# The gate's sigmoids and the exponentials' table load issued with the gate's sums, and head 1's transposes one unit later, in a hybrid decoder layer on one core

## The chip, the cores and the metric

The kernel runs on one core of one Trainium2 chip. The metric is device time in microseconds (us), the median of several runs; less is better. Beside the runs stands one profiled execution, from which every row of the trace in this document comes. Engines are called as in the profile: PE (TensorE's matmuls), PEld (its weight loads), DVE (VectorE), ACT (ScalarE), POOL (GpSimd), SP (SyncE, which here only issues DMAs).

## The reference, cut to what matters

One decoder layer on 256 tokens of width 1024, all in float32:

```python
h = rms_norm(x, norm1_g)
q, k, v, u = split(h @ w_in)               # 512 + 512 + 512 + 1024 columns
q, k = rope(rms_norm(q)), rope(rms_norm(k))
attn = softmax(mask(q k^T / 8)) v          # 8 heads of 64, causal
a, g = split(u + glu_b)                    # 512 + 512
c = causal_depthwise_conv(a * sigmoid(g))  # 31 taps, + dw_b
c = silu(layer_norm(c))
x = x + concat(attn, c) @ w_out
h = rms_norm(x, norm2_g)
y = x + (silu(h @ w_gate) * (h @ w_up)) @ w_down   # 2816 wide
```

With 256 tokens there is a single attention block, so the selection of blocks selects nothing.

## The kernel before, in words

Matmuls run in fp32r on split numbers. Each weight piece (128 x 1024, `raw`) is split in two: ACT copies it to `wh` (the high part, L289) and DVE subtracts that from it to get `wl` (the low part, L294). A product is three matmuls, high by high, high by low and low by high. SP loads the `raw` pieces in order, and a load waits for its buffer's release by the `wl` before it.

The first projection, `h @ w_in`, is tiled in 5 chunks of 512 columns (k, q, gate g, conv a, v) by 8 row tiles. One row tile of one chunk is a unit: 6 matmuls of 128 x 512 (L745), two token tiles of three products. So there are 40 units; units 25 to 32 belong to chunk 3 (the conv branch a), and a piece of weights serves two units. Each chunk accumulates in two PSUM banks `p`.

The order of the program is the order in which Python issues it, engine by engine. Everything but the projection's matmuls is written as generators, called tasks. Before each unit, `step()` resumes all tasks that are due, in the order in which they were spawned, and `feed()` issues the next `wh` and `wl`. `yield n` means: go on n units later; `yield 0` goes on in the same call. So these numbers decide what stands ahead of what in each engine's queue. The tasks that matter here:

- `spectra_task` (L444): three small matmuls `pw` on PE, one unit apart, each evicted by ACT to `Ws` (L455).
- `gate_task` (L597), spawned when the gate's chunk is done: DVE makes `ug` from the two banks (L602), then after a `yield` ACT does two sigmoids to `sgt` (L606). The next line (L607) is an exponential of a single column, whose purpose is that the table of the exponentials is loaded there.
- `pairs_task` (L545): the scores S of four heads on PE (L554), their mask and maximum on DVE (L562), and the bias `bi` from that (L566). It runs twice, for heads 0 to 3 and 4 to 7.
- `head_task` (L571), one for each head: two exponentials on ACT with the row sums (L576); for an odd head, one unit later, the reciprocal of the sums of a pair and the scaling of both heads' p on DVE (L583, L587); after another `yield` (L590, which reads `LATE` and `EVEN_T`) three transposes `pT` on PE (L593) and their eviction `pTs` on ACT (L595). The transposes use two PSUM banks in turn.
- `conv_task` (L609): `ua`, the folded sums and their split `hh`, `hl` on DVE and ACT (L615 to L629), and the spectrum `hf` on PE (L641, with the matmuls of `mm3` at L312 to L314).

After the projection follow attention times v (`O`, L764), the inverse transform and layer norm (`ln_task`), the output projection (`po`) and the feed-forward layer, whose matmuls are at L781.

`LATE` and `EVEN_T` are:

```python
EVEN_T = (4, 3, 4, 3)
LATE = (5,)
```

Of the kernel before, what the change touches and what calls it, by code (L numbers as in the profile page):

```python
# [39 lines left out]
HF_WAIT = 3  # L40
LN_WAIT = 2
EVEN_T = (4, 3, 4, 3)
Y_ENG = lambda nc: nc.vector
CV_FIRST = 1
WRAP_WAIT = 1
# [9 lines left out]
QT_WAIT = 2  # L55
KT_WAIT = 3
S_WAIT = 4
LATE = (5,)
SECOND = 3
SCORES = 8  # L60
SCRATCH = 8192
# [145 lines left out]
def _build(nc, tc, t, ctx):  # L207
# [12 lines left out]
    def t_bank(name, tag="t"):  # L220
        return psum.tile([P, 512], F32, name=name, tag=tag, bufs=2)

    def work(name, tag, bufs, shape=(P, W), dt=F32):
        return early.tile(list(shape), dt, name=name, tag=tag, bufs=bufs)
# [346 lines left out]
    def head_task(h):  # L571
# [9 lines left out]
        if h % 2:  # L581
# [7 lines left out]
            p = unscaled[h]  # L589
        yield (3 if h in LATE else 2) if h % 2 else EVEN_T[h // 2]  # L590
        b = t_bank(f"pT{h}")
# [5 lines left out]
    def gate_task(banks):  # L597
        G["sg"] = early.tile([P, NT, W], F32, name="sgt", tag="sg")
        us = []
        for i in range(NT):  # L600
            u = work(f"ug{i}", "tmp", 6)
            nc.vector.scalar_tensor_tensor(u, banks[i], rstd1[:, i:i + 1], G["glub"][:, 1, :], op0=ALU.mult, op1=ALU.add)  # L602
            us.append(u)
        yield 2
        for i in range(NT):
            nc.scalar.activation(G["sg"][:, i, :], us[i], AF.Sigmoid)  # L606
        nc.scalar.activation(table, one, AF.Exp)  # L607

    def conv_task(banks):  # L609
# [36 lines left out]
        for j in range(2):  # L646
            pa, pb = (work(f"y{a}{j}", "tmp", 6) for a in "ab")
            nc.vector.tensor_tensor(pa, hf[0], Ws[:, j, :], op=ALU.mult)
            nc.vector.tensor_tensor(pb, hf[1], Ws[:, 1 - j, :], op=ALU.mult)
            Y_ENG(nc).tensor_tensor(Y[j], pa, pb, op=(ALU.subtract, ALU.add)[j])  # L650

# [77 lines left out]
    spawn(tables_task(), CG_STEP)  # L729
    spawn(spectra_task(), SPECTRA)  # L730
    after = (k_task, q_task, gate_task, conv_task, None)
    unit = 0
    for chunk in range(5):
# [357 lines left out]
```

## Time and profile before

| | us |
|---|---|
| median of 3 runs | 281.49 (281.35 to 281.60) |
| profiled execution | 281.06 |
| its span, first to last instruction | 279.3 |
| PE busy | 273.8 |
| DVE busy | 240.4 |
| ACT busy | 189.5 |

The clock granted to TensorE was 1.000 over the span. A row of the timeline has the start and the duration in us, the engine, the line, the operation, output and inputs, shapes, and the count of instructions that are merged in it (x2); in brackets the idle time of the engine before it and what released it. A row of the waits reads: who waited for whom, us in total, how often, the longest. A row of the windows has the stretch, its length, then the busy time of PE, PEld, DVE, ACT and POOL with counts, the granted clock, the DMA share and GB/s.

### The profile page before, as it was taken

The numbers are of one execution on the slowest core, as the hardware profiler recorded it, in microseconds if no ns is written. First come the engines' busy times: TensorE is split into PE (matmuls) and PEld (weight loads), VectorE is DVE, ScalarE is ACT, GpSimd is POOL, SyncE is SP. The second block draws the span as 40 slices with busy tenths as digits, with TensorE's granted clock in tenths as the row PEclk, the third lists the DMA queues.
The fourth block names the chain that finished last, engine by engine and source line by source line (L and its number), as shares of the span: only waits on it lengthen the run. The fifth ranks groups of instructions, "written<-read, shape, count | busy, mean of one in ns | idle before, by whom it ended". The sixth has DMA issues, their size and how long they took to land.

```text
span 279.3 us, 3699 instructions
## 1 busy us (share of the span) xinstructions
PE 273.8 (98%) x1298; PEld 223.8 (80%) x1298; DVE 240.4 (86%) x346; ACT 189.5 (68%) x280; POOL 31.8 (11%) x59
## 2 busy tenths in 40 slices
PE   8999999899999999999999999999999999999995
PEld 5788877688788888888888888888888888888884
DVE  4999998899889957999998999899998999978412
ACT  4967767999769778655887469766687468954300
POOL 0005465002000000011200112002110022000000
PEclk9999999999999999999999999999999999999999
DMA  7999968565506887439999699997599985910012
GB/s 234 393 420 350 410 226 239 182 217 170 228 0 242 336 323 305 180 134 221 253 301 347 224 223 193 367 425 204 98 199 426 394 159 97 329 50 0 2 50 100
DMA packets 13378, 64.59 MB, mean 231 GB/s; under 512 B 1776, under 2 KB 2768, under 8 KB 7856
## 3 DMA queue, kind: packets, MB, share of 16 engines
q1 hardware_dynamic: 10144, 54.80, 51.5%
q0 software_dynamic: 2928, 9.43, 18.8%
q8 instruction: 10, 0.16, 0.2%
q10 hardware_dynamic: 288, 0.14, 0.2%
q14 instruction: 8, 0.07, 0.1%
HBM read 63.05 MB, written 1.05 MB: 230 GB/s over the span
## 4 chain that ended last, share of the span: by engine, by line
PE 94%; ACT 3%; DMA 1%; DVE 1%; issue 0%
PE pd L781 21%; PE p L745 18%; PE U L781 16%; PE fg L781 12%; PE po L781 8%; PE V L781 8%; PE W L781 4%; PE aT L862 2%; DMA first<-w 1%; PE pT L593 1%; PE O L764 1%; ACT p L576 1%; ACT wh L289 1%; PE x2T L804 1%; PE S L554 1%; ACT L607 0%
## 5 line engine op out<-in xcount | busy, mean ns | idle before, releaser
L289 ACT ACTIVATE wh<-raw 128x1024 fp32r<-128x1024 f32 x114 | 118.0, 1057 | 37.1 <-DVE raw L288 19.9
L294 DVE TENSOR_TENSOR wl<-raw,wh 128x1024 fp32r<-128x1024 f32 x114 | 136.1, 1221 | 6.5 <-ACT wh L289 5.6
L781 PE MATMUL pd<-wh,act 128*128 128x512 f32 (+1 forms) x176 | 57.2, 390 | 0.0
L781 PEld LDWEIGHTS pd<-wh,act 128*128 128x128 f32 x176 | 32.9, 188 | 6.6
L781 PE MATMUL pd<-wl,act 128*128 128x512 f32 (+1 forms) x88 | 33.9, 386 | 0.0
L745 PE MATMUL p<-wh,xh 128*128 128x512 f32 x80 | 32.5, 406 | 0.2 <-ACT wh L375 0.2
L302 POOL DMA_DIRECT2D raw<-w x16 | 14.0, 876 | 155.5 <-PE fg L781 58.5
L745 PE MATMUL p<-wh,xl 128*128 128x512 f32 x80 | 31.4, 393 | 0.0
L781 PE MATMUL fg<-wh,g 128*128 128x512 f32 x96 | 30.4, 391 | 0.0
L745 PE MATMUL p<-wl,xh 128*128 128x512 f32 x80 | 26.2, 390 | 0.0
L781 PE MATMUL U<-wh,g 128*128 128x512 f32 x64 | 21.5, 393 | 0.0
L781 PEld LDWEIGHTS fg<-wh,g 128*128 128x128 f32 x96 | 18.0, 188 | 3.7
L288 DVE TENSOR_TENSOR raw<-raw,raw 128x1024 f32<-128x1024 f32 x16 | 19.5, 1221 | 0.1
L781 PEld LDWEIGHTS pd<-wl,act 128*128 128x128 f32 x88 | 16.6, 188 | 3.2
L781 PE MATMUL fg<-wl,g 128*128 128x512 f32 x48 | 18.7, 390 | 0.0
L745 PEld LDWEIGHTS p<-wh,xh 128*128 128x128 f32 x80 | 15.0, 188 | 4.5 <-ACT wh L375 1.2
L745 PEld LDWEIGHTS p<-wh,xl 128*128 128x128 f32 x80 | 15.0, 188 | 3.3 <-DVE xl L370 0.4
L745 PEld LDWEIGHTS p<-wl,xh 128*128 128x128 f32 x80 | 15.0, 188 | 3.2
L865 ACT ACTIVATE act<-aT 128x512 fp32r<-128x512 f32 (+1 forms) x12 | 6.7, 560 | 12.9 <-PE aT L862 12.9
L781 PEld LDWEIGHTS U<-wh,g 128*128 128x128 f32 x64 | 12.0, 188 | 2.4
L781 PE MATMUL po<-wh,mixh 128*128 128x512 f32 x32 | 12.6, 395 | 0.0
L781 PE MATMUL po<-wh,mixl 128*128 128x512 f32 x32 | 12.5, 390 | 0.0
(202 smaller groups left out, 442.5 us busy)
## 6 DMA issues: line engine op xcount, KB each, us to landing
raw<-w SPq DMA_DIRECT2D x43, 1024.0 KB, 7.1
raw<-w POOLq DMA_DIRECT2D x16, 512.0 KB, 6.9
first<-w SPq DMA_DIRECT2D x8, 384.0 KB, 6.3
raw<-w SPq DMA_DIRECT2D x4, 512.0 KB, 7.0
xtok<-xtok SPq DMA_DIRECT2D x2, 512.0 KB, 8.3
x<-xtok SPq DMA_DIRECT2D x1, 1024.0 KB, 8.4
out<-o SPq DMA_DIRECT2D x3, 256.0 KB, 2.0
c_glub<-glub SPq DMA_DIRECT2D x1, 512.0 KB, 11.6
```

What stands on the lines that cost most here:

```text
L288: nc.vector.tensor_tensor(src, src, blocks[add][:, cut(a)], op=ALU.add)
L289: nc.scalar.activation(dst[0], src, AF.Copy)
L294: nc.vector.tensor_tensor(dst[1], src, dst[0].bitcast(F32), op=ALU.subtract)
L302: nc.gpsimd.dma_start(blocks[to][:, cut(a)], t["w"][HEAD + more - 2][:, cut(a)], accum_op=ALU.add)
L554: nc.tensor.matmul(banks[2 * j + a][:, out], G["qT"][rows, j, q], G["kT"][rows, j, k], start=True, stop=True)
L576: nc.scalar.activation(p[:, spl[i]], sm[:, spl[i]], AF.Exp, bias=bi[:, i:i + 1], scale=scq[:, i, h:h + 1], accum_out=s[:, i:i + 1])
L593: nc.tensor.transpose(b[:, a * P:(a + 1) * P], p[:, a * P:(a + 1) * P], ident)
L745: nc.tensor.matmul(banks[i], (xh, xh, xl)[a][:, kt, sls[i]], w[a % 2], start=kt == 0 and a == 0, stop=kt == KT - 1 and a == 2 - (order[-1] ...
L764: nc.tensor.matmul(o, vs[:, i, h * HD:(h + 1) * HD], G["pT"][h][:, i * T:i * T + T - i * P], start=i == 0, stop=i == 1)
L781: nc.tensor.matmul(bank, l, r, start=start and a == 0, stop=stop and a == 2, skip_group_check=on)
L862: nc.tensor.transpose(b[:, a, :], u[:, a * P:(a + 1) * P], ident)
L865: nc.scalar.activation(hi, b[:, 0:nf, :], AF.Copy)
```

## The change

Two numbers change, one by way of a new name:

```diff
+GLU_Y = 0
...
-LATE = (5,)
+LATE = (1, 5)
...
             us.append(u)
-        yield 2
+        yield GLU_Y
         for i in range(NT):
             nc.scalar.activation(G["sg"][:, i, :], us[i], AF.Sigmoid)
         nc.scalar.activation(table, one, AF.Exp)
```

With `GLU_Y = 0` the gate task doesn't pause between its sums on DVE and its sigmoids on ACT: they are issued in the same unit instead of two units later. With 1 in `LATE`, head 1 pauses 3 units instead of 2 ahead of its transposes (L590). The new name moves every line behind it by one: L606 is L607 in the changed kernel.

On ACT, around the gate task, these rows stood in the queue before (`Ws` are the tap spectra, `wh15` to `wh17` weight pieces, `sgt` the sigmoids, `p0` and `p1` the exponentials of heads 0 and 1):

```order
L455 ACTIVATE Ws_511<-pw0_512 128x512
L455 ACTIVATE Ws_511<-pw1_527 128x512
L289 ACTIVATE wh15_542<-raw7_303 128x1024
L455 ACTIVATE Ws_511<-pw2_552 120x512
L606 ACTIVATE sgt_516<-ug0_517 128x512
L606 ACTIVATE sgt_516<-ug1_519 128x512
L607 ACT_TABLE_LOAD
L607 ACTIVATE table_77<-one_75 128x1
L576 ACTIVATE p0_591,sums_515<-sm0_560,bi0_559,scq_438 128x128
```

On ACT, at the same place, with the change:

```order
L456 ACTIVATE Ws_511<-pw0_512 128x512
L607 ACTIVATE sgt_516<-ug0_517 128x512
L607 ACTIVATE sgt_516<-ug1_519 128x512
L608 ACT_TABLE_LOAD
L608 ACTIVATE table_77<-one_75 128x1
L456 ACTIVATE Ws_511<-pw1_530 128x512
L290 ACTIVATE wh15_545<-raw7_303 128x1024
L456 ACTIVATE Ws_511<-pw2_555 120x512
L577 ACTIVATE p0_591,sums_515<-sm0_560,bi0_559,scq_438 128x128
```

The four instructions of the gate move ahead of the second `Ws`, of `wh15` and of the third `Ws`; what follows them stands as it stood.

On PE, at the last unit of chunk 3 (`p30` and `p31` are its banks; `pT1` and `pT0` the transposes of heads 1 and 0), before:

```order
L745 MATMUL p31_510<-wl15_543,xh_110 128x512
L593 MATMUL pT1_668<-c_ident_168,p1_621 128x128 x3
L745 MATMUL p30_509<-wh15_542,xh_110 128x512
L745 MATMUL p30_509<-wl15_543,xh_110 128x512
L745 MATMUL p30_509<-wh15_542,xl_111 128x512
L745 MATMUL p31_510<-wh15_542,xh_110 128x512
L745 MATMUL p31_510<-wl15_543,xh_110 128x512
L745 MATMUL p31_510<-wh15_542,xl_111 128x512
L593 MATMUL pT0_688<-c_ident_168,p0_591 128x128 x3
```

On PE, at the same place, with the change:

```order
L746 MATMUL p31_510<-wl15_546,xh_110 128x512
L746 MATMUL p30_509<-wh15_545,xh_110 128x512
L746 MATMUL p30_509<-wl15_546,xh_110 128x512
L746 MATMUL p30_509<-wh15_545,xl_111 128x512
L746 MATMUL p31_510<-wh15_545,xh_110 128x512
L746 MATMUL p31_510<-wl15_546,xh_110 128x512
L746 MATMUL p31_510<-wh15_545,xl_111 128x512
L594 MATMUL pT0_682<-c_ident_168,p0_591 128x128 x3
L594 MATMUL pT1_688<-c_ident_168,p1_621 128x128 x3
```

The unit's six matmuls now stand ahead of all six transposes, and head 0 comes before head 1. DVE, POOL and SP have the same rows in the same order.

## The prediction

> **What bounds the kernel now.** I read the page first, then the waits of PE, then the timeline of the three engines around the one long wait. The forecast is 1.2 us less, worked out below.
>
> ```profile
> span 279.3 us, 3699 instructions
> PE 273.8 (98%) x1298; PEld 223.8 (80%) x1298; DVE 240.4 (86%) x346; ACT 189.5 (68%) x280; POOL 31.8 (11%) x59
> PE 94%; ACT 3%; DMA 1%; DVE 1%; issue 0%
> PE warm L359 <- DVE one L341: 1.0, 1, 1.0
> PE pT L593 <- DVE p L587: 0.8, 1, 0.8
> PE p L745 <- ACT wh L375: 0.2, 1, 0.2
> PEld O L764 <- ACT vs L752: 0.4, 1, 0.4
> ```
>
> PE is busy for 98% of the span and the chain that ended last is 94% PE, so time is won only where PE stands still. It waits three times as a matmul engine; two of them are in the start, which the change doesn't touch. The third, 0.83 us, is the wait of the first probability transposes (pT, of head 1) for DVE's scaling of p. The last row is a wait of the weight loads alone, near 71.8 us.
>
> PE around that wait, and two places where transposes follow without one (start, duration, operation):
>
> ```profile
> 53.18 0.61 PE L745 MATMUL p<-wl,xh 128*128 128x512 f32 x2
> 54.63 0.70 PE L593 MATMUL pT<-c_ident,p 128*128 128x128 f32 x3 [0.83 <-DVE p L587]
> 55.40 0.39 PE L745 MATMUL p<-wl,xh 128*128 128x512 f32 x1
> 55.63 0.40 PE L745 MATMUL p<-wh,xl 128*128 128x512 f32 x1
> ...
> 56.32 0.40 PE L745 MATMUL p<-wh,xl 128*128 128x512 f32 x1
> 56.56 0.49 PE L593 MATMUL pT<-c_ident,p 128*128 128x128 f32 x3
> 57.12 0.39 PE L745 MATMUL p<-wl,xh 128*128 128x512 f32 x1
> ...
> 58.05 0.40 PE L745 MATMUL p<-wh,xl 128*128 128x512 f32 x1
> 58.29 0.82 PE L593 MATMUL pT<-c_ident,p 128*128 128x128 f32 x6
> 59.17 0.40 PE L745 MATMUL p<-wl,xh 128*128 128x512 f32 x1
> ```
>
> Why p came late is read from ACT and DVE before it:
>
> ```profile
> 40.30 0.60 ACT L455 ACTIVATE Ws<-pw 128x512 f32<-128x512 f32 x1
> 41.95 0.60 ACT L455 ACTIVATE Ws<-pw 128x512 f32<-128x512 f32 x1 [1.05 <-PE pw L454]
> 42.45 1.05 ACT L289 ACTIVATE wh<-raw 128x1024 fp32r<-128x1024 f32 x1
> 45.28 0.60 ACT L455 ACTIVATE Ws<-pw 120x512 f32<-120x512 f32 x1 [1.78 <-PE pw L454]
> 45.78 1.15 ACT L606 ACTIVATE sgt<-ug 128x512 f32<-128x512 f32 x2
> 46.93 1.28 ACT L607 ACT_TABLE_LOAD   x1
> 48.22 0.20 ACT L607 ACTIVATE table<-one 128x1 f32<-128x1 f32 x1
> 48.33 0.48 ACT L576 ACTIVATE p<-sm,bi,scq 128x128 f32<-128x128 f32 x1
> 49.39 1.05 ACT L289 ACTIVATE wh<-raw 128x1024 fp32r<-128x1024 f32 x1
> 51.40 1.99 ACT L289 ACTIVATE wh<-raw 128x1024 fp32r<-128x1024 f32 x2
> ```
>
> ```profile
> 40.02 1.40 DVE L602 SCALAR_TENSOR_TENSOR ug<-p,c,c_glub 128x512 f32<-128x512 f32 x2
> 45.23 0.17 DVE L566 SCALAR_TENSOR_TENSOR bi<-mx,scq 128x8 f32<-128x8 f32 x1
> 45.31 1.22 DVE L294 TENSOR_TENSOR wl<-raw,wh 128x1024 fp32r<-128x1024 f32 x1
> 47.51 0.29 DVE L562 CUSTOM_DVE_ANT_0 sm<-S,c_mask 128x128 f32<-128x128 f32 x1 [0.98 <-PE S L554]
> 49.85 0.17 DVE L566 SCALAR_TENSOR_TENSOR bi<-mx,scq 128x8 f32<-128x8 f32 x1
> 50.47 1.23 DVE L294 TENSOR_TENSOR wl<-raw,wh 128x1024 fp32r<-128x1024 f32 x1 [0.45 <-ACT wh L289]
> 52.48 1.23 DVE L294 TENSOR_TENSOR wl<-raw,wh 128x1024 fp32r<-128x1024 f32 x1 [0.78 <-ACT wh L289]
> 53.62 0.17 DVE L583 RECIPROCAL rec<-sums 128x4 f32<-128x4 f32 x1
> 53.83 1.01 DVE L587 TENSOR_SCALAR p<-p,rec 128x128 f32<-128x128 f32 x4
> 57.01 0.75 DVE L615 SCALAR_TENSOR_TENSOR ua<-p,c,c_glub 128x512 f32<-128x512 f32 x1
> ```
>
> ACT is idle for 1.05 and 1.78 us between 40.9 and 45.28, waiting for the tap spectra (pw), although the gate's sums (ug) are ready at 41.42. Then it does sigmoids, table load and a dummy exponential, 2.55 us from 45.78 to 48.33, while the scores' bias of the first four heads lies ready since 45.40. The two wh behind the exponentials come late, DVE idles 0.45 and 0.78 us for them, and the reciprocal and the scaling behind those on DVE make PE wait.
>
> **The change part by part: the sigmoids and the table load.** They cost no new instruction: the same four move ahead of the second Ws, piece 15's wh and the third Ws. In the new place the first sigmoid starts at 40.30 + 0.50 (the step from 45.28 to 45.78) = 40.8; the second needs ug at 41.42 and starts near 41.5; at the rows' durations the load runs from 42.1 and the next instruction starts near 43.5. So the second Ws goes from 41.95 to 43.5, wh 15 from 42.45 to 44.0, ending at 45.05. Who waits for these: DVE's wl at 45.31, so 0.26 us is left, and behind that DVE has 0.98 us of idle before the second masks, whose start PE sets. The third Ws stays at 45.28 (PE released it), and the first exponential starts at 45.78, not 48.33: 2.55 us earlier. The second bias, 49.85 + 0.17 = 50.02, is in time for the third head (earlier by 2.55 too, at 50.75). No DMA is issued in the moved code, and SP and POOL keep their order.
>
> DVE then: the wh of pieces 16 and 17, at 49.39 and 51.40, start at 46.84 and 48.85. The wl start at 50.02 and, 1.13 later, 51.15, neither waiting; the reciprocal at 52.28 instead of 53.62, 1.34 us earlier; the scalings at 52.49. Before, the first pT started 0.80 us after the scalings did (53.83 to 54.63), so now one could start at 53.29.
>
> **Its worth on PE.** I measure by starts. The last p matmul before the wait started at 53.18 + 0.22 = 53.40 (two in 0.61, one 0.39), the second one after it at 55.40: 2.00 us. The same stretch with three transposes and no wait is 56.32 to 57.12: 0.80. So the wait costs 1.20 us, not 0.83: the 0.37 more is the emptying and refilling of the array. The Trainium skill (Perfetto Trace Analysis, Tensor Engine Instruction) says that a matmul's end is estimated by the profiler and its start observed. By ends the sum would be 0.83 and the forecast 280.7; by starts it is 1.20, and the trace backs the starts, as the two stretches above differ by 1.20.
>
> **Head 1's transposes a unit later.** Without a wait PE would leave unit 31 at 53.40 + 0.23 = 53.63 (the step is 55.40 to 55.63). Now six matmuls stand first, and pT is reached at 53.63 + 6 x 0.23 = 55.01. With p ready at 53.29, that cover is 1.72 us; without this edit it would be 0.34 us. So I cost the edit at nothing: either part alone removes the wait at this place. Six transposes together instead of twice three: 58.05 to 59.17 is 1.12 us, less two steps of 0.23 is 0.66; singly 0.80 - 0.46 = 0.34, twice 0.68. That is 0.02 saved. ACT must empty both banks before heads 2 and 3, which come at 58.29 - 1.20 = 57.09; the evictions end near 56.3.
>
> **What is late next.** PE comes 1.20 us earlier to everything behind. DVE's next dense stretch must come along:
>
> ```profile
> 56.00:72.00 16.00, 16.00 (x83) 13.03 (x83) 15.65 (x33) 14.75 (x34) 1.99 (x4) 1.00 0.62 220
> 63.38 1.29 DVE L629 TENSOR_TENSOR hl<-uf,hh 128x512 fp32r<-128x512 f32 x2
> 65.33 0.39 PE L313 MATMUL hf<-hl,fwd 128*128 128x512 f32 x1
> ```
>
> DVE is busy 15.65 of 16 us there (third number). It needs PE for ua, at 57.01 before and 55.67 now; chunk 3 ends on PE near 55.2. So it keeps its 1.34 us. The nearest margin is hl: ready at 64.67, used at 65.33, 0.66 us; now 0.66 + 1.34 - 1.20 = 0.80. After 72 us PE shows no wait at all, so the 1.20 us should reach the end.
>
> **The sum.** Profiled execution: 281.06 (span 279.3 and 1.76 around it), less 1.20, is 279.86. It lies 0.43 below the median of the runs, 281.49; from that the forecast is 280.29, so 280.3. The bounds: 0.37 us more if the weight loads' wait at 71.8 goes with ACT's lead (279.9); 0.83 instead of 1.20 if the refill is hidden elsewhere (280.7).
>
> **The rivals.** *DVE stays where it is.* If wh 17 ends after 52.4 as before, the idle 1.23 us survives. Head 1's later place still removes the wait, but hl is then 0.54 us late for PE (0.66 - 1.20), and with 0.37 of refill 0.91 comes back: 281.2. For it: ACT is 14.75 of 16 us busy behind. Against it: it needs wh 17 2.5 us later than worked out.
>
> *Slower: the moved block holds up wh 15.* If wh 15 ended at E, DVE would lose E - 46.29 us (47.51 - 1.22). PE waits for hl when that exceeds 0.80, with 0.37 of refill; the gain of 1.20 is eaten at a loss of 1.63, E = 47.9, against 45.05. At E = 48.8 it is 281.49 - 1.20 + (2.5 - 0.8 + 0.37) = 282.4. The rows speak against it: the table load took 1.28 and the dummy started behind it at once. The Trainium skill (ScalarE: Activation LUTs, What ACT_TABLE_LOAD costs) puts a drain of 1.38 us beside the load; the trace shows none. By that E would be 46.4 and DVE would lose 0.1 us, which the margin of 0.80 covers.
>
> *Half of it:* refill not won or a small wait at heads 2 and 3: 280.7.
>
> **How the numbers follow.** A measurement of this kernel tells 0.2% from no change, 0.56 us. Forecast 280.3: 0.63; half of it: 0.17; DVE stays: 0.13; slower: 0.07. So faster 0.80, same 0.13, slower 0.07. The range runs from the bound 279.9 to the unchanged-DVE case at 281.2 and holds more than 8 in 10.
>
> **What would show it.** Right: the first exponential near 45.8, the DVE reciprocal near 52.3, no idle before pT, six pT in a row near 55.0, and the same steps behind 1.2 us earlier. Wrong: a new PE wait for hl (L313), for pT of heads 2 and 3, or in the FFN; a wl at 45.31 that waits for ACT; or a span shorter by 0.8 or less with no PE idle left.

## The result, and the profile after

| | before | changed |
|---|---|---|
| median, us | 281.45 (7 runs) | 279.97 (7 runs) |
| ratio of the runs | | 0.995 (95% interval 0.9936 to 0.9964) |
| profiled execution | 281.06, span 279.3 | 280.43, span 278.6 |

The change makes the kernel faster by 1.48 us in the medians, 1.0 to 1.8 us by the interval. The forecast was 1.2 us and 280.3. Three executions among the runs of the experiments below (345.8, 396.3 and 463.6 us, at mean granted clocks of 0.76, 0.66 and 0.56) count in the medians, which they move by less than 0.1 us, and not in the ratios.

From the page of the changed kernel, the span, the busy times and the chain that ended last, and from its waits all that PE itself waited for, and the weight loads' wait near 71 us:

```profile
span 278.6 us, 3702 instructions
PE 274.1 (98%) x1298; PEld 224.8 (81%) x1298; DVE 240.2 (86%) x346; ACT 189.4 (68%) x280; POOL 31.7 (11%) x59
PE 96%; DMA 2%; ACT 0%; SPq 0%; DVE 0%; issue 0%; ACTq 0%
```

```profile
PE warm L360 <- DVE one L342: 1.0, 1, 1.0
PEld O L765 <- ACT vs L753: 0.4, 1, 0.4
```

The wait for p is gone and no other has taken its place. (The 0.2 us that PE waited in the start before the change is absent too, but `glu_only` and `late_silu` below have it again.) ACT and DVE have left the chain but for fractions of a per cent.

Rows from the timeline of ACT in the changed kernel, at the moved block (line numbers are one higher than before, and rows in between are left out here and in the next two):

```profile
40.86 0.60 ACT L456 ACTIVATE Ws<-pw 128x512 f32<-128x512 f32 x1
41.35 1.15 ACT L607 ACTIVATE sgt<-ug 128x512 f32<-128x512 f32 x2
42.50 1.28 ACT L608 ACT_TABLE_LOAD   x1
44.38 1.05 ACT L290 ACTIVATE wh<-raw 128x1024 fp32r<-128x1024 f32 x1
45.84 0.60 ACT L456 ACTIVATE Ws<-pw 120x512 f32<-120x512 f32 x1 [0.41 <-PE pw L455]
46.34 0.49 ACT L577 ACTIVATE p<-sm,bi,scq 128x128 f32<-128x128 f32 x1
```

That of DVE:

```profile
45.87 1.22 DVE L295 TENSOR_TENSOR wl<-raw,wh 128x1024 fp32r<-128x1024 f32 x1
50.50 2.36 DVE L295 TENSOR_TENSOR wl<-raw,wh 128x1024 fp32r<-128x1024 f32 x2
52.77 0.17 DVE L584 RECIPROCAL rec<-sums 128x4 f32<-128x4 f32 x1
```

And that of PE:

```profile
53.74 0.62 PE L746 MATMUL p<-wl,xh 128*128 128x512 f32 x2
55.33 0.40 PE L746 MATMUL p<-wh,xl 128*128 128x512 f32 x1
55.56 0.82 PE L594 MATMUL pT<-c_ident,p 128*128 128x128 f32 x6
56.45 0.39 PE L746 MATMUL p<-wl,xh 128*128 128x512 f32 x1
57.61 0.82 PE L594 MATMUL pT<-c_ident,p 128*128 128x128 f32 x6
```

This execution was already 0.56 us later than that of before when it got here (53.74 against 53.18), so steps are compared from there. On the clock of the trace before, the exponentials start at 45.78 (46.34 less 0.56), as forecast, against 48.33; the two wl follow each other without a wait; the reciprocal comes at 52.21 (forecast 52.28); and the second matmul behind head 0's transposes, at 57.12 before, is at 56.45, which is 0.67 earlier on the bare clock and 1.23 earlier from the unit ahead of the wait. The forecast of the step was 1.20 + 0.02. The spans differ by 0.7 us, which with the 0.56 is 1.26: what was won here reached the end.

### The profile page after: what moved, and what is told of

It is laid out like the page before. It is cut to its first block, busy times and chain, and to the rows that moved or that the text cites. A ratio compares the mean times of both kernels' runs of the same rounds, so it can differ in the third digit from the quotient of the medians.

```text
span 278.6 us, 3702 instructions
## 1 busy us (share of the span) xinstructions
PE 274.1 (98%) x1298; PEld 224.8 (81%) x1298; DVE 240.2 (86%) x346; ACT 189.4 (68%) x280; POOL 31.7 (11%) x59
## 3 DMA queue, kind: packets, MB, share of 16 engines
HBM read 63.05 MB, written 1.05 MB: 230 GB/s over the span
## 4 chain that ended last, share of the span: by engine, by line
PE 96%; DMA 2%; ACT 0%; SPq 0%; DVE 0%; issue 0%; ACTq 0%
PE pd L782 21%; PE p L746 19%; PE U L782 16%; PE fg L782 12%; PE po L782 8%; PE V L782 8%; PE W L782 4%; DMA first<-w 2%; PE aT L863 2%; PE S L555 1%; PE O L765 1%; PE pT L594 1%; PE x2T L805 1%; PE cT L722 0%; PE pdlast L782 0%; PE qT L498 0%
```

## The experiments

Each edit is against the changed kernel unless it says otherwise, and each time is against runs of the kernel before on the same chip: with the first four runs a median of 281.51, with the next two 281.25, with the last four 281.27.

**Each part alone.** `glu_only`, the gate's part:

```diff
-LATE = (1, 5)
+LATE = (5,)
```

> Only the gate's part of the change: sigmoids and table load in the same unit, head 1's transposes where they stood. My theory (either part alone removes PE's wait, this one because DVE also gets 1.34 us ahead): the whole gain, 1.2 us less than before, no PE wait at the first pT, a cover of about 0.3 us there. Rival (the later transposes are needed): a wait of some tenths stays at pT and the gain is 0.5 us or less.

Measured: 279.84 us, ratio 0.9944 (0.993 to 0.9958). PE doesn't wait at pT, which starts at 53.78, 1.25 us after DVE began the scalings (52.53). The whole gain is here, and the rival is wrong.

`late_only`, head 1's part:

```diff
-GLU_Y = 0
+GLU_Y = 2
```

> Only head 1's later transposes; the sigmoids two units behind the gate's sums as before. My theory: the wait at pT is gone, but ACT and DVE are not ahead, so hl is ready at 64.67 on the clock of the trace before while PE comes for it at 64.13: a new PE wait of 0.54 us there and 0.37 us of refilling, net gain 0.3 us (0.1 to 0.5). Rival (this part alone does it): 1.2 us less than before and no wait at hf.

Measured: 281.07 us, ratio 0.9993 (0.998 to 1.0005), at most 0.6 us less than before. The size fits my theory, but by luck, since the place does not. The timeline of PE with this part alone, at hf and at the transposes of heads 6 and 7:

```profile
63.68 0.48 PE L313 MATMUL hf<-hh,fwd 128*128 128x512 f32 x1
64.08 0.50 PE L314 MATMUL hf<-hl,fwd 128*128 128x512 f32 x1
64.42 0.40 PE L315 MATMUL hf<-hh,fwd 128*128 128x512 f32 x1
...
67.86 0.39 PE L746 MATMUL p<-wh,xl 128*128 128x512 f32 x1
68.86 0.93 PE L594 MATMUL pT<-c_ident,p 128*128 128x128 f32 x6 [0.61 <-ACT pTs L596]
...
69.86 0.39 PE L746 MATMUL p<-wl,xh 128*128 128x512 f32 x1
```

And that of ACT there:

```profile
65.98 1.28 ACT L580 ACT_TABLE_LOAD   x1
...
67.39 1.04 ACT L290 ACTIVATE wh<-raw 128x1024 fp32r<-128x1024 f32 x1
68.33 0.85 ACT L596 ACTIVATE pTs<-pT 128x384 f32<-128x384 f32 x2
```

At hf the steps are 0.40 and 0.34 us instead of 0.32 and 0.22 as in the trace before: 0.2 us. The larger loss is later. From the last p matmul to the second one behind six transposes is 2.00 us (67.86 to 69.86) against 1.12 without a wait: 0.88. The transposes of heads 6 and 7 need the two banks of heads 4 and 5, and ACT begins to empty those only at 68.33, behind the load of the silu's table and a wh. Together 1.1 of the 1.2 us is lost again.

**Who holds the gain back there?** `late_silu` is `late_only` with the silu's load moved out of that queue:

```diff
 head_task:
-        if h == H - 1:
-            nc.scalar.activation(table, one, AF.Silu)
...
 ln_task:
+        nc.scalar.activation(table, table, AF.Silu)
         yield CV_WAIT
```

> Head 1's later transposes alone, and the load of the silu's table moved from behind the last exponentials (ACT, L579 before) to the layer norm, where ACT idled 2.7 us. In the run with the later transposes alone PE waited at the transposes of heads 6 and 7 for ACT's evictions of heads 4 and 5, 0.8 us by starts, and 0.2 us at hf. Theory (ACT's queue behind the exponentials holds the gain back): the load's 1.4 us leave that queue, the wait at heads 6 and 7 goes, 0.2 us at hf stays, and it is 1.0 us less than before. Rival (DVE's hl holds it, and the wait at heads 6 and 7 only follows from it): still 0.3 us less than before.

Measured: 279.88 us, ratio 0.9953 (0.9938 to 0.9968). ACT's timeline at the same place:

```profile
65.60 1.04 ACT L290 ACTIVATE wh<-raw 128x1024 fp32r<-128x1024 f32 x1
66.55 0.84 ACT L594 ACTIVATE pTs<-pT 128x384 f32<-128x384 f32 x2
68.34 0.87 ACT L594 ACTIVATE pTs<-pT 128x384 f32<-128x384 f32 x2 [0.95 <-PE pT L592]
```

The evictions of heads 4 and 5 now start at 66.55, ACT idles 0.95 us for PE where PE had waited for ACT, and the gain is there with DVE as late as before. So ACT's queue was the holder, and DVE's hl cost only its 0.2 us or a little more.

**One unit instead of none.** `glu_one`:

```diff
-GLU_Y = 0
-LATE = (1, 5)
+GLU_Y = 1
+LATE = (5,)
```

> The gate's sigmoids one unit behind its sums instead of two or none, head 1's transposes where they stood; the block then stands behind the second Ws and ahead of piece 15's wh. My theory: the block fills idle time from about 42.5 to 45.0, wh 15 goes to about 45.0 and ends near 46.1, the exponentials start near 46.6 instead of 48.3, which is early enough: 1.2 us less than before. Rival (only the foremost place is early enough): less than half of it.

Measured: 279.91 us, ratio 0.9952 (0.9934 to 0.9971). The first exponential starts at 46.36 (forecast 46.6). The foremost place is not needed.

**A longer block in the new place.** `sig3`:

```diff
+        for _ in range(3):
+            nc.scalar.activation(G["sg"][:, 1, :], us[1], AF.Sigmoid)
         nc.scalar.activation(table, one, AF.Exp)
```

> The changed kernel with the second sigmoid done three times more, which adds 3 x 0.52 = 1.57 us to ACT's block ahead of the second Ws and piece 15's wh (the result is the same). My theory: wh 15 ends near 46.6 on the clock of the trace before, DVE's wl waits 1.3 us for it, but the 0.98 us of idle ahead of the second masks and the margin of 0.8 us at hl take it: no time lost against the changed kernel, 1.2 us less than before. Rival (every microsecond in front of wh 15 counts): 1.6 us slower than the changed kernel, 0.4 us slower than before.

Measured: 280.36 us, ratio 0.996 (0.9946 to 0.9974). The trace comes from a second set of runs of the same kernel, `sig3_again`:

> The changed kernel with the second sigmoid done three times more, again, for its profile. The repeats take 1.96 us, not 1.57, so wh 15 ends 2.0 us later and DVE's second masks start 0.3 to 0.8 us later. Theory: the margins at the first pT (1.7 us) and at hl (0.8 us) take it, so no wait of over 0.3 us on PE, and 0.9 to 1.2 us less than before. Rival (every microsecond in front of wh 15 counts): 0.8 us slower than before.

Measured: 280.41 us, ratio 0.9966 (0.9952 to 0.998): 0.96 us less than before by the ratio. The three repeats took 1.96 us, 0.65 each, where the two sigmoids ahead of them step at 0.52 (two in 1.14, one 0.62). The repeats all write the same half of `sgt` and those two write different halves; whether that is the reason was not tested. DVE's wl for piece 15 in this run, then PE around the transposes of heads 6 and 7:

```profile
47.55 1.22 DVE L295 TENSOR_TENSOR wl<-raw,wh 128x1024 fp32r<-128x1024 f32 x1 [1.50 <-ACT wh L290]
...
68.39 0.39 PE L748 MATMUL p<-wh,xl 128*128 128x512 f32 x1
68.74 0.92 PE L594 MATMUL pT<-c_ident,p 128*128 128x128 f32 x6
...
69.73 0.40 PE L748 MATMUL p<-wl,xh 128*128 128x512 f32 x1
```

The wl waits 1.50 us for wh 15. On PE, behind the start, only the stretch at heads 6 and 7 is longer, 1.34 us (68.39 to 69.73) instead of 1.12. Two microseconds in front of wh 15 cost these 0.2 us by the trace and some 0.4 by the ratios, whose intervals overlap: the margins take most of it.

`pair`, a further pair of table loads:

```diff
         nc.scalar.activation(table, one, AF.Exp)
+        nc.scalar.activation(table, one, AF.Sigmoid)
+        nc.scalar.activation(table, one, AF.Exp)
```

> The changed kernel with one more pair of table loads behind the gate's (a sigmoid and an exponential of one column, each with its load: 2 x (1.28 + 0.2) = 2.97 us more ahead of the second Ws and piece 15's wh; the result is the same). My theory: DVE loses 1.6 us by then (2.56 us later at wl 15, less the 0.98 us of idle), the transposes of the first heads are just covered, and at hl the margin of 0.8 us is overrun by 0.8 us: with 0.37 us of refilling 1.2 us slower than the changed kernel, about the time of before. Rival 1 (all of it is hidden): the time of the changed kernel. Rival 2 (each switch of tables costs 2.66 us, 1.38 more than its load's row): DVE loses 4.3 us and the kernel is 3 us slower or more than before.

Measured: 281.50 us, ratio 1.0008 (0.9996 to 1.0019), the time of before, which is the number of my theory. ACT's timeline in this run, the three loads up to the second Ws:

```profile
42.94 1.28 ACT L608 ACT_TABLE_LOAD   x1
44.24 0.20 ACT L608 ACTIVATE table<-one 128x1 f32<-128x1 f32 x1
44.46 1.28 ACT L609 ACT_TABLE_LOAD   x1
...
45.98 1.28 ACT L610 ACT_TABLE_LOAD   x1
47.27 0.20 ACT L610 ACTIVATE table<-one 128x1 f32<-128x1 f32 x1
47.38 0.58 ACT L456 ACTIVATE Ws<-pw 128x512 f32<-128x512 f32 x1
```

From load to load is 1.52 us, the load and its dummy, with no drain between. The Trainium skill (ScalarE: Activation LUTs, What ACT_TABLE_LOAD costs) puts 1.38 us of drain beside each; neither this trace nor the time has room for two more of those. PE's loss of 1.2 us is again mostly at the transposes of heads 6 and 7: a wait of 0.64 us for ACT's evictions, 0.9 by starts (69.08 to 71.11 instead of 1.12). At hf and the transposes ahead of it, where I had put all of it, it is 0.3 (64.22 to 65.91 instead of 1.35). That the number came out is luck in part.

**The same block in the old place.** Against the kernel before, the second sigmoid once, twice and three times more (`sig1_old`, `sig2_old`, `sig3_old`):

```diff
+        for _ in range(n):
+            nc.scalar.activation(G["sg"][:, 1, :], us[1], AF.Sigmoid)
         nc.scalar.activation(table, one, AF.Exp)
```

> The kernel before with the second sigmoid done three times more, 1.57 us more ahead of the exponentials (the result is the same). My theory: there the block stands on the path, so PE's wait at the first pT grows from 0.83 to 2.4 us and the kernel is 1.6 us slower than before. Rival (the wait has another cause, a wh or a load): no change, or less than 0.8 us.

> The kernel before with the second sigmoid done once more: 0.65 us more ahead of the exponentials, by the run with three more (which took 1.96 us). Theory (slope of one, and the granted clock falls only after a long wait): PE's wait at the first pT is 1.5 us, the clock stays at 1.0, 0.65 us slower than before. Rival (a wait of more than 0.83 us already costs the clock): 1.5 us slower or more, matmuls behind it at 0.43 us a step.

> The kernel before with the second sigmoid done twice more: 1.3 us more ahead of the exponentials. Theory: PE waits 2.1 us at the first pT. Without a fall of the clock it is 1.3 us slower than before, with one as in the run with three more 2.7 to 3.0 us slower. I expect no fall (1.3), the wait being under 2.5 us.

| added on ACT, us | PE's wait at pT, us | median, us | ratio |
|---|---|---|---|
| 0 | 0.83 | 281.25, 281.27 | 1 |
| about 0.65, once | 1.50 | 282.08 | 1.0023 (1.0011 to 1.0034) |
| about 1.3, twice | 2.16 | 283.57 | 1.0083 (1.0056 to 1.0109) |
| 1.96, three times | 2.83 | 284.89 | 1.0131 (1.0112 to 1.0149) |

The wait grows by what is added, to within 0.05 us: here the block stands on the path, where the changed kernel swallows the same 1.96 us. The first row behind zero costs 0.65 us by its ratio. With three the loss is 3.6 us, far over my 1.6. PE in that run, and two of its windows (the granted clock is the third number from the end):

```profile
56.93 0.70 PE L594 MATMUL pT<-c_ident,p 128*128 128x128 f32 x3 [2.83 <-DVE p L588]
57.39 0.50 PE L748 MATMUL p<-wh,xh 128*128 128x512 f32 x1
57.72 0.60 PE L748 MATMUL p<-wl,xh 128*128 128x512 f32 x1
58.12 0.63 PE L748 MATMUL p<-wh,xl 128*128 128x512 f32 x1
58.54 0.63 PE L748 MATMUL p<-wh,xh 128*128 128x512 f32 x1
```

```profile
58.00:61.00 3.00, 3.00 (x10) 2.31 (x10) 2.93 (x9) 1.44 (x3) 0.00 (x0) 0.50 0.71 298
62.00:66.00 4.00, 4.00 (x22) 3.35 (x21) 3.50 (x9) 4.00 (x12) 0.18 (x1) 1.00 0.73 258
```

Behind the wait the matmuls step at 0.42 us instead of 0.23 (58.12 to 58.54), the granted clock is 0.50 from 58 to 61 us, and from 62 us it is 1.00 again. From 57.72 to 61.24 the steps exceed the usual ones by 1.6 us together, which with 2.0 of wait makes the 3.6. All four runs of this kernel have a mean granted clock of 0.992 to 0.994. With two repeats, two of four runs have 0.993 (283.91 and 284.78 us) and two 0.998 and 1.0 (282.61 and 283.24): a wait of 2.16 us costs the clock in some executions and not in others, and my expectation of no fall was half right. With one, the nine runs that count in the ratio stand at 0.998 to 1.0. Only one run of each kernel has a trace (for two repeats it is the one of 282.61 us, whose clock stays at 1.00 there); for the others the fall is read from the mean clock and the time.

## Why the prediction was right, point by point

- *What bounds the kernel*: right. Only PE's standing time counted, and the chain went from 94% to 96% PE.
- *The moved block costs nothing*: right; the first exponential 2.55 us earlier to the hundredth, wl 15 without a wait. Its cover was about as large as I said (0.26 + 0.98 + 0.80 = 2.04 us): 1.96 us more cost 0.2 us by starts and some 0.4 by the ratios, at heads 6 and 7 and not at hl.
- *DVE 1.34 us ahead*: right, 52.21 for 52.28.
- *A wait costs the starts, not the ends*: 1.23 us measured from start to start where the idle column says 0.83. The medians' interval, 1.0 to 1.8 us, holds 1.23 and leaves out 0.83. I put the 0.37 in between down to the emptying and refilling of the array. The rows before show where it lies, not that cause. The last matmul ahead of the wait lasts 0.39 us where the usual step is 0.23. The three transposes take 0.45 us to the next start (54.63 to 55.08) instead of 0.24 (56.56 to 56.80). That is 0.16 + 0.21. The second part goes with the weight loads of the transposes, which need p: behind the wait they start with the transposes, without a wait 0.24 us ahead of them. The two rows, from the timeline of PEld before:

```profile
54.63 0.46 PEld L593 LDWEIGHTS pT<-c_ident,p 128*128 128x128 f32 x3 [1.25 <-DVE p L587]
56.32 0.48 PEld L593 LDWEIGHTS pT<-c_ident,p 128*128 128x128 f32 x3
```

- *The lower bound, 279.9, if the weight loads' wait at 71.8 goes*: it didn't go, it is 0.4 us after as before. The median is 0.3 us under the forecast all the same. The traces, compared from the unit ahead of the wait, give 1.26, and no run says where the rest of the 1.48 is; the interval holds both.
- *Head 1's part is worth nothing beside the gate's*: right, 279.84 without it and 279.97 with it. *Either part alone removes the wait at this place*: right too, but alone head 1's part is worth little.
- *The nearest margin is hl*: wrong. It is the eviction of heads 4 and 5 ahead of the transposes of heads 6 and 7. I had checked that pair of banks only for heads 0 to 3. In the trace before ACT began those evictions at 68.45 and PE its next transposes at 69.23; with 0.48 us for one eviction the first bank was free at 68.93, a margin of 0.30, under the 0.66 of hl. The forecast held because ACT came ahead as well, by 1.40 us there (67.61 less 0.56, against 68.45), for which the prediction had no term at that place: that much was luck.
- *The rival in which DVE stays, at 281.2*: `late_only` is that case, at 281.07 and with ACT's evictions instead of hl as the holder.
- *The slower rival*: its break-even was an ACT block 2.9 us longer (47.9 against 45.05); `pair`, with 2.97 more, gave the time of before, though not by a wait for hl alone.

## What to carry to other kernels

Price a wait of PE by the starts of the matmuls around it against an undisturbed stretch of the same kind; the idle column left out a third here. An engine that idles for one producer while work further back in its queue lies ready, as ACT did here for 1.05 and 1.78 us, is worth a look at the order of its queue. Whether the lead helps is decided by every later meeting of the two engines, PSUM banks waiting for eviction included. Postponing only the consumer gained little here, since the producer's queue stayed as late and met it again.

## What the runs showed of the hardware

PE's granted clock fell after a wait of 2.83 us in four of four runs and after one of 2.16 us in two of four, and not after 1.50 in nine of nine; in the one trace that shows a fall it was 0.50 from 58 to 61 us. The Trainium skill (TensorE: Matmul & The Clock Gate, The HAM clock gate) gives an idle window of about 3.4 us that runs freely; the runs agree that it depends on the execution, but the fall came after shorter waits than that (by the matmuls' starts the two are 3.2 and 2.6 us). Why one execution falls and another doesn't, no run here shows.

Matmul steps of 0.42 us, as behind the long wait, also stand at the start. Early matmuls of the changed kernel's profile, then of the profile before:

```profile
5.17 0.63 PE L746 MATMUL p<-wh,xl 128*128 128x512 f32 x1
5.59 0.63 PE L746 MATMUL p<-wh,xh 128*128 128x512 f32 x1
6.02 0.53 PE L746 MATMUL p<-wh,xl 128*128 128x512 f32 x1
```

```profile
4.98 0.50 PE L745 MATMUL p<-wh,xl 128*128 128x512 f32 x1
5.32 0.40 PE L745 MATMUL p<-wh,xh 128*128 128x512 f32 x1
5.55 0.39 PE L745 MATMUL p<-wh,xl 128*128 128x512 f32 x1
```

The steps are 0.42 and 0.43 us in the changed kernel and 0.34 and 0.23 before. That the clock comes up at another moment in each execution fits this, but isn't shown: the granted clock reads 1.00 from 4 to 7 us in both profiles. The next wl matmul starts at 6.39 in the changed kernel and at 5.78 before, which is the 0.56 us, and a little more, by which the two profiles were apart before the change had any effect. In the traces of the experiments it starts between 5.72 and 6.50. A gain of 1 us is not to be read from two spans alone.
